# One channel tile of a depthwise convolution: its products on ScalarE instead of GpSimd

## The chip, the cores and the metric

The kernel runs on one core of one Trainium2 chip. The metric is the device time of one execution in microseconds, as the median of several runs. The engines go by the profile's names: PE is TensorE, PEld its weight loads, ACT is ScalarE, DVE is VectorE, POOL (Pool) is GpSimd, SP the engine that issues the transfers.

## What is computed

A two-layer decoder trunk over 1024 tokens of 1024 channels. Layer 0 mixes tokens with a causal convolution module, layer 1 with a gated DeltaNet; behind each mixer stands an MLP with a squared ReLU. The change touches only the convolution of layer 0:

```python
def conformer_conv(h, w_pw1, b_pw1, w_dw, b_dw, ln_g, ln_b, w_pw2, b_pw2):
    u = h @ w_pw1 + b_pw1
    u = jax.nn.glu(u, axis=-1)
    u = causal_depthwise_conv(u, w_dw) + b_dw      # width 31, each channel by itself
    u = jax.nn.silu(layer_norm(u, ln_g, ln_b))
    return u @ w_pw2 + b_pw2

for i in range(DEPTH):
    h = h + mix(rms_norm(h, norm_mix_g[i]))
    h = h + sqrelu_mlp(rms_norm(h, norm_ffn_g[i]), mlp_w1[i], mlp_w2[i])
```

## The kernel before

**Tiles.** Channels stand on the 128 partitions, in 8 channel tiles; the 1024 tokens are done in two halves of 512 (half 0 and half 1). A dense product makes one 128x512 output tile: 8 steps over the input channels, each of three matmuls (L200, L201, L202), because weights and activations are split into a high and a low part (wh, wl; hi, lo) to keep float32's precision. So a product is 24 matmuls. ACT makes the high part of a weight tile (L160), DVE the low part (L161); each of them has two buffers, and the transfers are issued two products ahead, at raised priority (L215).

**The work around the change.** While half 1's convolution runs on DVE, Pool and ACT, PE runs the first MLP of half 0, in four quarters q = 0 to 3 of 8 hidden products (named m1_qo, in full m1_00_qo) and 8 output products (m2_qo). Behind a hidden product, ACT does a ReLU (L573), a square (L574) and the high part of the split (L99), and DVE the low part (L100). Behind an output product, DVE scales (L604, into xo) and adds to h (L357). After the MLP, half 1's second pointwise product (pw2, ps_p) needs the convolution's layer norm.

**The convolution of half 1.** A table, CONV (L30), names for each half and channel tile who does it. A tile of kind "v" is done on DVE alone: 31 multiply-adds (L498), accumulated in PSUM. Kinds "p" and "a" are done by conv_pool (L418): ACT writes the first tap into the sum (L427, cp); then come 30 products of a tap with the shifted input, and 30 adds into the sum on Pool (L437). For "p" the products (cv) are made by Pool (L432), for "a" by ACT (L435). The second number of an entry is the pace: after how many taps the generator yields. In half 1, tiles 0, 1 and 7 go by conv_pool, one after the other; tiles 2 to 6 go by conv_vec on DVE. The products' tiles come from one pool of 27 buffers (GB, L42), which they share with other temporaries.

**What follows a tile.** When a tile is done, conv_done (L405) adds it into a running sum on DVE (L415, ln). When all are, the layer norm (L510) takes the mean over channels with a matmul (L240, mean_lnm), subtracts it on DVE (L519), squares on ACT (L271) and adds up on Pool (L523), takes another matmul (L530, lnv) for the variance, and then 1/sqrt (L246 on ACT, L247 on DVE), a scaling (L542 on DVE, L540 on Pool), Silu twice a tile on ACT (L550, L551) and a split on DVE (L552). Its output tiles (la) share 17 buffers (AB, L41) with the 8 tiles of the MLP's input and 8 hidden tiles, so that all of them are to be had only when the last hidden product of q = 3 has been made.

**What sets the order.** The generators of convolution and layer norm are advanced twice for each dense product (tick, L168). But the order in which each engine gets its instructions is set by the framework's scheduler (the option at L46): it plays the whole program through on a cost model of its own and writes each engine's instructions down in the order in which they would run in it. On the chip each engine keeps to that order, whatever the durations are there. So an edit to one table entry can move instructions on all engines.

Of the kernel before, what the change touches and what calls it, by code (L numbers as in the profile page):

```python
# [27 lines left out]


CONV = ((("a", 2), ("a", 2), ("v", 1), ("v", 2), ("a", 2), ("v", 1), ("s", 1), ("t", 1)),  # L30
        (("p", 1), ("p", 1), ("v", 3), ("v", 1), ("v", 1), ("v", 3), ("v", 1), ("p", 3)))
SHARED = 8
DIAG = 16
WB = 2
# [1184 lines left out]
```

## Time and profile before

| | us |
|---|---|
| median of 3 runs | 2414.03 (2412.52 to 2415.59) |
| the profiled execution | 2410.71 |
| its span in the trace | 2409.0 |
| mean granted clock of PE | 0.986 |
| Pool's work on half 1's convolution ends | 609.45 |
| first matmul of m2_30 (the last hidden product of half 0's first MLP is done) | 607.33 |
| first matmul of half 1's pw2 | 661.63 |

All times in the trace count from the start of the span. A row of the timeline has the start, the duration, engine, line, operation, the tile written and the tiles read, the count if several equal ones follow each other, and in brackets how long the engine had been idle before and what released it. Matmuls overlap their ends, so that the distance of two starts, and not the duration, is the price of one. "Granted clock" is the share of full speed that the clock gate gave PE.

### The profile page before, as it was taken

To read this page: it belongs to the slowest core of one execution; us is meant where nothing else is said; L and a number is where in the kernel's file an instruction comes from. 1 tells how busy PE (TensorE), PEld (TensorE's weight loads), DVE (VectorE), ACT (ScalarE), POOL (GpSimd) and SP (SyncE) were. 2 spreads that over 40 slices of the span, in tenths; PEclk is the share of its full clock that TensorE was granted. 3 is DMA by queue.
4 is the path that set the end of the run, shared out by engine and by line. 5 is a ranking of instruction groups with operands and counts; after the bars stand their busy time and mean duration, and the time that the engine had idled before them with its cause. 6 is when DMAs were issued, how large, how long until landed. Compare 5 with 4: busy or idle time off the path is not lost. (4 is left out here: it accounts for less than half of the span.)

```text
span 2409.0 us, 30448 instructions
## 1 busy us (share of the span) xinstructions
PE 2335.2 (97%) x11484; PEld 1930.9 (80%) x11484; DVE 1594.6 (66%) x2637; ACT 1069.9 (44%) x1566; POOL 574.3 (24%) x414
## 2 busy tenths in 40 slices
PE   8899999999999989999999999899999999999998
PEld 6687778888778878888888888788888887888888
DVE  5797999545868978667444689786775446533334
ACT  6862443243546554352424365544524244432342
POOL 5981399999400110110000000101000000000000
PEclk9898999999999999999999999999999999999999
DMA  8744222333334534333344345343333343433332
GB/s 295 242 166 152 93 88 89 103 96 97 127 114 145 175 112 135 113 120 96 100 140 138 124 138 181 116 128 119 120 97 101 126 132 101 131 96 97 97 104 79
DMA packets 121028, 302.67 MB, mean 126 GB/s; under 512 B 29552, under 2 KB 31792, under 8 KB 120880
## 3 DMA queue, kind: packets, MB, share of 16 engines
q1 hardware_dynamic: 120880, 300.73, 39.0%
q8 instruction: 90, 1.47, 0.3%
q14 instruction: 58, 0.48, 0.1%
HBM read 252.41 MB, written 48.27 MB: 125 GB/s over the span
## 5 line engine op out<-in xcount | busy, mean ns | idle before, releaser
L160 ACT ACTIVATE wh_m<-raw_m 128x1024 fp32r<-128x1024 f32 x256 | 271.4, 1061 | 761.0 <-PE ps_m L201 680.3
L161 DVE TENSOR_TENSOR wl_m<-raw_m,wh_m 128x1024 fp32r<-128x1024 f32 x256 | 327.4, 1279 | 221.2 <-ACT wh_m L160 213.2
L202 PE MATMUL ps_m<-hid,wl_m 128*128 128x512 f32 (+1 forms) x1088 | 414.1, 382 | 10.0 <-DVE wl_m L161 10.0
L200 PE MATMUL ps_m<-hid,wh_m 128*128 128x512 f32 (+1 forms) x1088 | 413.8, 381 | 1.3 <-ACT wh_m L160 0.5
L201 PE MATMUL ps_m<-hid,wh_m 128*128 128x512 f32 (+1 forms) x1088 | 412.1, 380 | 0.0
L437 POOL TENSOR_TENSOR cp<-cp,cv 128x512 f32<-128x512 f32 x187 | 275.4, 1480 | 10.9 <-ACT cv L435 3.7
L202 PEld LDWEIGHTS ps_m<-hid,wl_m 128*128 128x128 f32 x1088 | 205.7, 189 | 49.8 <-DVE wl_m L161 13.4
L200 PEld LDWEIGHTS ps_m<-hid,wh_m 128*128 128x128 f32 x1088 | 205.7, 189 | 39.1 <-ACT wh_m L160 1.8
L201 PEld LDWEIGHTS ps_m<-hid,wh_m 128*128 128x128 f32 x1088 | 205.6, 189 | 36.7 <-issue 0.2
L200 PE MATMUL ps_m<-xn_b,wh_m 128*128 128x512 f32 x512 | 201.4, 393 | 1.0 <-ACT wh_m L160 1.0
L200 PE MATMUL ps_m<-xn_a,wh_m 128*128 128x512 f32 x512 | 200.9, 392 | 1.2 <-ACT wh_m L160 1.2
L201 PE MATMUL ps_m<-xn_a,wh_m 128*128 128x512 f32 x512 | 200.8, 392 | 0.0
L202 PE MATMUL ps_m<-xn_a,wl_m 128*128 128x512 f32 x512 | 200.7, 392 | 0.0
L201 PE MATMUL ps_m<-xn_b,wh_m 128*128 128x512 f32 x512 | 200.6, 392 | 0.0
L202 PE MATMUL ps_m<-xn_b,wl_m 128*128 128x512 f32 x512 | 200.4, 392 | 0.0
L498 DVE SCALAR_TENSOR_TENSOR ca<-u,vec,ca 128x512 f32<-128x512 f32 x268 | 186.1, 743 | 0.4
L432 POOL TENSOR_SCALAR cv<-u,vec 128x512 f32<-128x512 f32 x90 | 174.5, 1946 | 0.0
L1006 POOL TENSOR_TENSOR fof<-fof,rstd_f 128x256 f32<-128x256 f32 x3 | 2.6, 889 | 580.7 <-DVE rstd_f L999 580.7
L800 POOL TENSOR_TENSOR ld<-qe,ld 128x512 f32<-128x512 f32 x16 | 21.6, 1348 | 449.6 <-DVE e L775 274.6
L100 DVE TENSOR_TENSOR hid<-mt,hid 128x512 fp32r<-128x512 f32 x128 | 94.2, 736 | 43.4 <-ACT hid L99 43.2
L200 PEld LDWEIGHTS ps_m<-xn_b,wh_m 128*128 128x128 f32 x512 | 96.2, 188 | 21.7 <-ACT wh_m L160 1.8
L200 PEld LDWEIGHTS ps_m<-xn_a,wh_m 128*128 128x128 f32 x512 | 96.2, 188 | 21.6 <-ACT wh_m L160 2.1
(373 smaller groups left out, 4723.2 us busy)
## 6 DMA issues: line engine op xcount, KB each, us to landing
raw_m<-w SPq DMA_DIRECT2D x256, 512.0 KB, 3.5
raw_in<-w_in SPq DMA_DIRECT2D x64, 512.0 KB, 3.6
sc<-iy SPq DMA_DIRECT2D x64, 256.0 KB, 2.2
ld<-sc SPq DMA_DIRECT2D x64, 256.0 KB, 3.9
raw_p<-w_pw SPq DMA_DIRECT2D x16, 512.0 KB, 3.6
raw_go<-w_out SPq DMA_DIRECT2D x16, 512.0 KB, 3.6
x<-x SPq DMA_DIRECT2D x24, 256.0 KB, 5.4
dh_pa<-wh_pa SPq DMA_DIRECT2D x8, 512.0 KB, 4.0
```

Source lines behind the costliest of these rows:

```text
L100: nc.vector.tensor_tensor(out=dst[:, 1, :], in0=src, in1=dst[:, 0, :].bitcast(F32), op=ALU.subtract)
L160: nc.scalar.activation(out=wh[:, s], in_=raw[:, s], func=AF.Copy)
L161: nc.vector.tensor_tensor(out=wl[:, s], in0=raw[:, s], in1=wh[:, s].bitcast(F32), op=ALU.subtract)
L200: nc.tensor.matmul(o, wh[:, s], hi, start=(k == 0), stop=False)
L201: nc.tensor.matmul(o, wh[:, s], lo, start=False, stop=False)
L202: nc.tensor.matmul(o, wl[:, s], hi, start=False, stop=last)
L432: nc.gpsimd.tensor_scalar(out=t, in0=u[:, j:j + HT], scalar1=tap(ct, j), scalar2=None, op0=ALU.mult)
L437: nc.gpsimd.tensor_tensor(out=c, in0=c, in1=t, op=ALU.add)
L498: nc.vector.scalar_tensor_tensor(out=c if j == CW - 1 else acc, in0=u[:, j:j + HT], scalar=tap(ct, j), in1=acc, op0=ALU.mult, op1=ALU.add)
L800: nc.gpsimd.tensor_tensor(out=qT[h], in0=qe, in1=qT[h], op=ALU.mult)
L1006: nc.gpsimd.tensor_tensor(out=y, in0=y, in1=r, op=ALU.mult)
```

## The change

One entry of CONV: half 1's tile 1 goes from ("p", 1) to ("a", 2). Its 30 products are made by ACT with L435 instead of Pool with L432; its 30 adds stay on Pool; conv_pool yields 15 times for the tile instead of 30. Tiles 0 and 7 stay as they are.

```diff
 CONV = ((("a", 2), ("a", 2), ("v", 1), ("v", 2), ("a", 2), ("v", 1), ("s", 1), ("t", 1)),
-        (("p", 1), ("p", 1), ("v", 3), ("v", 1), ("v", 1), ("v", 3), ("v", 1), ("p", 3)))
+        (("p", 1), ("a", 2), ("v", 3), ("v", 1), ("v", 1), ("v", 3), ("v", 1), ("p", 3)))
```

PE and DVE keep their numbers of instructions, ACT has 30 more and Pool 30 fewer. The order changes on all of them between the first MLP's second quarter and half 1's pw2, from where on it is that of before. Three places, the names read as above (cp1_7 is the convolution's sum of half 1, tile 7; the last number of a name counts instructions):

DVE of the kernel before, where it takes tile 7's sum over, late in q = 3:

```order
L161 TENSOR_TENSOR wl_m1_00_37_4787<-raw_m1_00_37_4784,wh_m1_00_37_4786 128x1024
L100 TENSOR_TENSOR hid_00_35_4780<-mt_00_35_4777,hid_00_35_4780 128x512
L161 TENSOR_TENSOR wl_m2_00_30_4826<-raw_m2_00_30_4823,wh_m2_00_30_4825 128x1024
L415 TENSOR_TENSOR ln1_3117<-ln1_3117,cp1_7_3780 128x512
L100 TENSOR_TENSOR hid_00_36_4819<-mt_00_36_4816,hid_00_36_4819 128x512
L415 TENSOR_TENSOR ln1_3117<-ln1_3117,c1_5_4062 128x512
L161 TENSOR_TENSOR wl_m2_00_31_4870<-raw_m2_00_31_4867,wh_m2_00_31_4869 128x1024
```

DVE of the changed kernel, where it takes the same sum over, in q = 2:

```order
L161 TENSOR_TENSOR wl_m2_00_22_4301<-raw_m2_00_22_4298,wh_m2_00_22_4300 128x1024
L604 TENSOR_TENSOR xo_00_21_4330<-ps_m2_00_21_4304,rstd_r2_2796 128x512
L161 TENSOR_TENSOR wl_m2_00_23_4337<-raw_m2_00_23_4334,wh_m2_00_23_4336 128x1024
L357 TENSOR_TENSOR h01_2147<-h01_2147,xo_00_21_4330 128x512
L415 TENSOR_TENSOR ln1_3117<-ln1_3117,cp1_7_3502 128x512
L604 TENSOR_TENSOR xo_00_22_4366<-ps_m2_00_22_4340,rstd_r2_2796 128x512
L415 TENSOR_TENSOR ln1_3117<-ln1_3117,c1_4_3374 128x512
L357 TENSOR_TENSOR h02_2182<-h02_2182,xo_00_22_4366 128x512
L161 TENSOR_TENSOR wl_m2_00_24_4373<-raw_m2_00_24_4370,wh_m2_00_24_4372 128x1024
```

The sum L415 of cp1_7 stood behind the weight split of m2_30 and ahead of that of m2_31; it now stands ahead of that of m2_24. PE's first matmul with that split is its row 2392 in the one case and 2081 in the other, of a numbering that counts alike in both.

ACT of the kernel before, in q = 1, from the weight split of m1_15 on:

```order
L160 ACTIVATE wh_m1_00_15_3322<-raw_m1_00_15_3320 128x1024
L573 ACTIVATE mt_00_13_3310<-ps_m1_00_13_3281 128x512
L574 ACTIVATE mt_00_13_3310<-mt_00_13_3310 128x512
L99 ACTIVATE hid_00_13_3313<-mt_00_13_3310 128x512
L160 ACTIVATE wh_m1_00_16_3371<-raw_m1_00_16_3369 128x1024
L573 ACTIVATE mt_00_14_3359<-ps_m1_00_14_3326 128x512
L574 ACTIVATE mt_00_14_3359<-mt_00_14_3359 128x512
L99 ACTIVATE hid_00_14_3362<-mt_00_14_3359 128x512
```

ACT of the changed kernel, ahead of and behind the weight split of m1_16:

```order
L574 ACTIVATE mt_00_13_3337<-mt_00_13_3337 128x512
L435 ACTIVATE cv1_1_29_3479<-u1_1_1374,vec_96 128x512
L99 ACTIVATE hid_00_12_3289<-mt_00_12_3286 128x512
L435 ACTIVATE cv1_1_30_3482<-u1_1_1374,vec_96 128x512
L427 ACTIVATE cp1_7_3502<-u1_7_2012,vec_96 128x512
L160 ACTIVATE wh_m1_00_16_3407<-raw_m1_00_16_3405 128x1024
L573 ACTIVATE mt_00_14_3392<-ps_m1_00_14_3356 128x512
L99 ACTIVATE hid_00_13_3340<-mt_00_13_3337 128x512
```

Between a square and a split of the MLP now stand products of tile 1, the last two of which are seen here, and the first tap of tile 7 (L427), directly ahead of the weight split of m1_16. The block of products begins behind the first tap of tile 1, where L574 of m1_11 stood: twelve products, that L574, four products, the weight split of m1_14, and so on. By the semaphores of the built program products 17 and 18 wait for the buffers that Pool's adds 1 and 3 of the tile free, and so on to product 30 (add 14) and the first tap of tile 7 (add 15).

ACT of the changed kernel, at the beginning of q = 3's output products:

```order
L551 ACTIVATE cp1_0_2434<-cp1_0_2434,vec_96 128x512
L551 ACTIVATE cp1_1_3119<-cp1_1_3119,vec_96 128x512
L551 ACTIVATE c1_2_2429<-c1_2_2429,vec_96 128x512
L551 ACTIVATE c1_3_2679<-c1_3_2679,vec_96 128x512
L551 ACTIVATE c1_4_3374<-c1_4_3374,vec_96 128x512
L551 ACTIVATE c1_5_4063<-c1_5_4063,vec_96 128x512
L551 ACTIVATE c1_6_4282<-c1_6_4282,vec_96 128x512
L160 ACTIVATE wh_m2_00_32_4911<-raw_m2_00_32_4909 128x1024
L551 ACTIVATE cp1_7_3502<-cp1_7_3502,vec_96 128x512
L160 ACTIVATE wh_m2_00_33_4953<-raw_m2_00_33_4951 128x1024
```

These are the second Silus of the layer norm (L551), behind the table load and the eight first Silus (L550), which follow L99 of the last hidden product; the weight split of m2_32 stands behind seven of them. In the kernel before the Silus stood behind the weight split of m2_36.

On Pool, the adds of tile 1 stood between its own products; now 17 of them stand one behind the other, and the later ones stand between products of tile 7.

## The prediction, made before the changed kernel was run

> **What bounds the kernel now.** I read the page's table of engines first, then the busy time by stretch over the part of the kernel that the change can reach.
>
> ```profile
> PE 2335.2 (97%) x11484; PEld 1930.9 (80%) x11484; DVE 1594.6 (66%) x2637; ACT 1069.9 (44%) x1566; POOL 574.3 (24%) x414
> 360.00:420.00 60.00, 60.00 (x266) 49.71 (x265) 60.00 (x82) 21.02 (x27) 58.82 (x35) 1.00 0.30 92
> 540.00:600.00 60.00, 60.00 (x266) 49.69 (x265) 33.52 (x32) 22.19 (x29) 59.30 (x35) 1.00 0.31 98
> 640.00:660.00 20.00, 15.11 (x58) 11.68 (x58) 19.00 (x26) 15.20 (x23) 2.31 (x2) 0.91 0.46 146
> ```
>
> In a row by stretch stand the stretch, its length, then busy time and count of PE, PEld, DVE, ACT and Pool, and the granted clock. TensorE is the bound: 97% of the span. Within the first MLP it is gapless (266 matmuls in 60 us, 0.226 us each, so one product of 24 takes 5.44 us). Pool is nearly full there too, while its work is no part of PE's bound; it matters only through who waits for it. PE loses time at 640 to 660. The timeline of PE shows where, and which of its waits DVE's wait for Pool causes:
>
> ```profile
> 542.50 0.39 PE L202 MATMUL ps_m<-hid,wl_m 128*128 128x512 f32 x1
> 607.33 0.39 PE L200 MATMUL ps_m<-hid,wh_m 128*128 128x512 f32 x1
> 611.44 1.12 PE L240 MATMUL mean_lnm<-ln,mean_w 128*128 128x512 f32 x2 [0.77 <-DVE ln L415]
> 643.89 0.39 PE L201 MATMUL ps_m<-hid,wh_m 128*128 128x512 f32 x1
> 646.51 0.50 PE L202 MATMUL ps_m<-hid,wl_m 128*128 128x512 f32 x1 [2.23 <-DVE wl_m L161]
> 651.86 0.40 PE L201 MATMUL ps_m<-hid,wh_m 128*128 128x512 f32 x1
> 654.91 0.69 PE L202 MATMUL ps_m<-hid,wl_m 128*128 128x512 f32 x1 [2.66 <-DVE wl_m L161]
> 655.41 0.63 PE L200 MATMUL ps_m<-hid,wh_m 128*128 128x512 f32 x1
> 655.83 0.63 PE L201 MATMUL ps_m<-hid,wh_m 128*128 128x512 f32 x1
> 658.39 0.43 PE L201 MATMUL ps_m<-hid,wh_m 128*128 128x512 f32 x1
> ```
>
> From 643.89 to 646.51 is 2.62 us where 0.23 was due, from 651.86 to 654.91 it is 3.05: 5.2 us lost. Then from 655.41 to 658.39 seven matmuls start 0.426 us apart, about 1.6 us more for the eight slow ones: 6.8 us in all at 640 to 660, while ScalarE and DVE finish the convolution's layer norm. The wait for the convolution itself (at 611.44) costs 0.8 us. So in the kernel before, Pool's half of the convolution is almost completely hidden. Pool's own rows, and DVE's where it takes Pool's last sum over:
>
> ```profile
> 350.43 1.57 POOL L432 TENSOR_SCALAR cv<-u,vec 128x512 f32<-128x512 f32 x1
> 351.96 1.29 POOL L437 TENSOR_TENSOR cp<-cp,cv 128x512 f32<-128x512 f32 x1
> 367.56 29.20 POOL L437 TENSOR_TENSOR cp<-cp,cv 128x512 f32<-128x512 f32 x16
> 396.75 24.54 POOL L432 TENSOR_SCALAR cv<-u,vec 128x512 f32<-128x512 f32 x14
> 477.33 3.05 POOL L432 TENSOR_SCALAR cv<-u,vec 128x512 f32<-128x512 f32 x1
> 583.03 26.42 POOL L437 TENSOR_TENSOR cp<-cp,cv 128x512 f32<-128x512 f32 x15
> L432 POOL TENSOR_SCALAR cv<-u,vec 128x512 f32<-128x512 f32 x90 | 174.5, 1946 | 0.0
> 609.49 0.69 DVE L415 TENSOR_TENSOR ln<-ln,cp 128x512 f32<-128x512 f32 x1 [5.30 <-POOL cp L437]
> 610.10 0.68 DVE L100 TENSOR_TENSOR hid<-mt,hid 128x512 fp32r<-128x512 f32 x1
> 610.70 0.68 DVE L415 TENSOR_TENSOR ln<-ln,c 128x512 f32<-128x512 f32 x1
> 611.30 1.22 DVE L161 TENSOR_TENSOR wl_m<-raw_m,wh_m 128x1024 fp32r<-128x1024 f32 x1
> ```
>
> Tile 1's work on Pool begins at 396.75 and tile 7's first product at 477.33. Pool ends at 583.03 + 26.42 = 609.45, and 0.04 us later DVE takes the sum, having waited 5.30 us for it, with a weight split (L161) three places behind.
>
> **What the change takes from Pool.** Thirty products L432 leave Pool, at a mean of 1.946 us: 58.4 us. In exchange the adds of tile 1 now wait for ScalarE. That engine's rows at the place:
>
> ```profile
> 401.31 0.62 ACT L574 ACTIVATE mt<-mt 128x512 f32<-128x512 f32 x1
> 410.04 1.06 ACT L160 ACTIVATE wh_m<-raw_m 128x1024 fp32r<-128x1024 f32 x1 [2.56 <-PE ps_m L201]
> 420.92 1.07 ACT L160 ACTIVATE wh_m<-raw_m 128x1024 fp32r<-128x1024 f32 x1 [2.57 <-PE ps_m L201]
> L435 ACT ACTIVATE cv<-u,vec x97: 707/711/725, 39.6 to 177.7; 128x512 f32<-128x512 f32 x97
> ```
>
> In the new order the first of these products stands right behind the start of tile 1's sum (L427), where L574 stood at 401.31. It takes 0.71 us (L435 of half 0), so Pool, free at 396.75, starts at 402.0: 5.3 us idle. Net 53.1 us, and Pool would end at 609.45 - 53.1 = 556.4. That is the value I take. The bounds: the stretch from 477.33 to 609.45 (30 products and 44 adds, 132.1 us) stays; ahead of it stand 16 adds, the number that shared the old stretch with tile 1's products. At 29.20/16 = 1.82 us each, as the row beside a busy DVE has them, they take 29.1 us and Pool ends at 402.0 + 29.1 + 132.1 = 563.2. At 1.29 us (the row at 351.96) they take 20.6 us, and if DVE, standing still in a wait, leaves the last fifteen adds at 1.29 instead of 26.42/15 = 1.76, 7 us more go: 547.7. The difference between the 1.29 and the 1.82 us is a busy DVE. The Trainium skill (GPSIMD Engine Reference, section 8, Key points) says that Pool shares its SBUF interfaces with VectorE and contends with DVE instructions that have two SBUF inputs; these rows agree, and by that rule alone the low end, 547.7, would be the likely one.
>
> **What it moves.** This is where the price lies. The new order brings DVE's sum of tile 7 (L415) forward, from behind the split for product m2_30 to a place ahead of the split for product m2_24; both stand as excerpts with the change. The matmul that needs this split is PE's row 2081, that of m2_31 is row 2392. At 0.2267 us (5.44/24) a row, the 311 rows are 70.5 us, so the demand on Pool comes 70.5 us earlier while Pool is done only 53.1 us earlier. In absolute times: the matmul ran at 542.50 (its row above: 607.33 is row 2367, less 286 rows). DVE needs, after Pool's end, the sum, an L604, another sum, an L357 and the split. By the rows at 609.49 to 611.30 each short one costs 0.60 us and the split 1.22: 0.04 + 4 x 0.60 + 1.22 = 3.7 us. With Pool's end at 556.4 the split is there at 560.1, and PE is 560.1 - 542.5 = **17.6 us** late. DVE processes in order, so the split has no way past the sum; PE, in order too, has no other product to go to. By the bounds: 547.7 gives 8.9 us, 563.2 gives 24.4.
>
> This lateness does not come in one piece. Earlier steps take parts of it, and what they take is then no longer waited for, since Pool's end does not hang on PE. (1) ScalarE: the order puts 16 products and an L574 ahead of the weight split wh of m1_14. From 401.3, 16 x 0.71 + 0.62 = 12.0 us on: it starts at 413.3 instead of 410.04, 3.3 us late. (2) The later products must wait for buffers that Pool's adds free, and the start of tile 7's sum (L427), which needs the buffer of add 15, stands directly ahead of wh of m1_16. Add 15 ends at 402.0 + 15 x 1.82 = 429.3 (421.4 at 1.29), and with 0.8 us for L427 and 1.07 for the split it is there at 431.2 where it was at 422.0: 9.2 us late, or 1.3 by the low price. DVE's split follows it. So PE is about 9 us late from product m1_16 on. (3) DVE's sums of tile 1 and its last steps for tile 4 to 6 are brought forward in the same way, ahead of the splits of m1_26 and m2_20, and wait for Pool's adds too. What remains is taken at m2_24. The sum of all is the 17.6 us, as long as Pool is the latest; if Pool were done by 548, the 9.2 us of ScalarE would be all.
>
> A wait of such length has a follow-up price. Behind the 2.66 us wait at 654.91 the matmuls ran at 0.426 us for eight pieces: 1.6 us, which I add once, behind the last of the waits (the earlier ones are absorbed). The Trainium skill (TensorE: Matmul & The Clock Gate, What's actually happening) has the half clock after an idle window of about 3.4 us; here 2.66 us was enough, so the row decides, and for the longer waits expected here both give the same.
>
> Removed: the 0.8 us wait at 611.44, since the layer norm is now past it by then.
>
> **The layer norm's end.** Its Silu batch can't move up: its tiles come free only with the last hidden product, which ends at PE's 607.33 (T0). In the kernel before the batch comes later and costs the 6.8 us at 640 to 660. ScalarE's rows of it:
>
> ```profile
> 608.27 0.58 ACT L573 ACTIVATE mt<-ps_m 128x512 f32<-128x512 f32 x1
> 609.55 0.63 ACT L99 ACTIVATE hid<-mt 128x512 fp32r<-128x512 f32 x1
> 639.28 1.28 ACT L550 ACT_TABLE_LOAD   x1
> 641.91 2.73 ACT L550 ACTIVATE la<-c,vec 128x512 fp32r<-128x512 f32 x4
> 648.32 2.12 ACT L551 ACTIVATE c<-c,vec 128x512 f32<-128x512 f32 x3
> ```
>
> The new order puts the table load and the first 15 Silus between L99 of m1_37 and wh of m2_32. The batch starts at T0 + 2.9 (609.55 + 0.63), takes 1.28 + 15 x 0.69 (2.73/4 and 2.12/3 lie around it) = 11.6, then the split 1.06: wh is there at T0 + 15.6. PE wants it two products after T0, at T0 + 10.9: about 4.7 us late, 0.5 us more for DVE's part (its split takes 1.22, of which two matmuls run beside it), and 1.6 at the half clock: 6.8 us. So this term is +6.8 - 6.8 = 0. One stall takes the place of the other.
>
> Sum: 17.6 + 1.6 - 0.8 + 0 = **+18.4 us**. The profiled execution is 2410.71 us (span 2409.0 and 1.7 around it), 3.3 us under the median of 2414.03; it would become 2429.1. On the median it is 2432.4. The bounds: 8.9 and 24.4 in place of 17.6 give +9.7 and +25.2, that is 2423.7 and 2439.2; 2 us on each side for the Silu term, which only my reading of the order gives, make 2421.7 to 2441.2.
>
> **Rivals.**
> - *Faster.* Pool runs at its undisturbed prices through the whole stretch: 30 x 1.57 + 44 x 1.29 = 103.9 instead of 132.1 us. Then it ends at 402.0 + 20.6 + 103.9 = 526.5, DVE never waits, and if the Silu batch is hidden as well, the 6.8 and the 0.8 us go: 2414.0 - 7.6 = 2406.4. It decides at a Pool end of 542.5 - 3.7 = 538.8. Against it: products of 3.05 us such as that at 477.33 and the mean of 1.946 stand in the very stretch, and ScalarE's block at m1_16 would also have to vanish. Chance 0.05.
> - *No change.* Pool ends before 538.8 and ScalarE's products fit in, but the Silu batch costs what it cost before: 2414.0 - 0.8 = 2413.2. For it: PE's waits for the convolution total 0.8 us, so there is little that could be won. Chance 0.06.
> - *Slower by ScalarE only.* Pool is done by 548, and the 9.2 us at m1_16 with 1.6 behind it are what counts: 9.2 + 1.6 - 0.8 = +10.0, 2424.0. For it: DVE standing still makes Pool quicker. The Trainium skill's rule on the shared interfaces (GPSIMD Engine Reference, section 8, Key points) speaks for this case. Chance 0.14.
>
> **How the numbers follow.** The forecast (DVE waits for Pool, 2432.4) has 0.75. The range 2422 to 2441 holds it and the third rival; what is left out is the two others, 0.11, and tails of the forecast. A measurement of this kernel can tell about 0.2%, 4.8 us, from no change: below 2409.2 is faster (0.05), up to 2418.9 the same (0.06), above it slower (0.89).
>
> **What would show it.** Right: Pool's last add at about 556 (548 to 563); ScalarE's L435 rows with waits for Pool, and its L160 at 410 and 421 late by 3 and 9 us; DVE's L415 and L498 waiting for Pool in several pieces at 500 to 560, and behind each PE's L202 waiting for DVE's L161 with 0.43 us matmuls after it; 17 to 18 us lost by the end of m2_24, and another 7 us some 11 us after the last hidden product, while the waits at 644 to 655 are gone. Wrong: Pool done before 539; or L415 waiting with PE undisturbed, which would mean that the splits are not behind it; or a loss after pw2 has begun, where the order of all engines is that of before.

## The result and the profile after

The changed kernel took 2435.32 us (median of 4 runs, 2434.89 to 2436.45) against 2413.28 us (4 runs) of the kernel before: a ratio of 1.0083 (95% interval 1.0071 to 1.0095), slower by 22.0 us. Forecast were 18.4 more, 2432.4 us. The profiled execution has a span of 2433.8 us. Each ratio below is against executions of the kernel before that were taken together with it (medians 2413.28 to 2413.97). The medians leave out two executions that ran slowly at a lower granted clock, one of pool_relief (0.912) and the profiled one of tile7_on_act (0.856), so that nothing is read from the latter's trace.

The page's engine row of the changed kernel:

```profile
PE 2344.6 (96%) x11484; PEld 1935.3 (80%) x11484; DVE 1598.0 (66%) x2637; ACT 1088.0 (45%) x1596; POOL 512.9 (21%) x384
```

Pool lost 574.3 - 512.9 = 61.4 us of work and ScalarE took up 18.1; PE, which does the same matmuls, ran slower. Where, the timelines of the changed kernel say. First ScalarE and Pool in q = 1, then Pool's end:

```profile
403.31 7.46 ACT L435 ACTIVATE cv<-u,vec 128x512 f32<-128x512 f32 x12
410.67 0.62 ACT L574 ACTIVATE mt<-mt 128x512 f32<-128x512 f32 x1
411.19 2.54 ACT L435 ACTIVATE cv<-u,vec 128x512 f32<-128x512 f32 x4
413.64 1.04 ACT L160 ACTIVATE wh_m<-raw_m 128x1024 fp32r<-128x1024 f32 x1
...
427.67 0.82 ACT L427 ACTIVATE cp<-u,vec 128x512 f32<-128x512 f32 x1 [0.41 <-POOL cp L437]
428.39 1.04 ACT L160 ACTIVATE wh_m<-raw_m 128x1024 fp32r<-128x1024 f32 x1
```

```profile
404.10 26.62 POOL L437 TENSOR_TENSOR cp<-cp,cv 128x512 f32<-128x512 f32 x17 [6.78 <-ACT cv L435]
...
532.72 25.41 POOL L437 TENSOR_TENSOR cp<-cp,cv 128x512 f32<-128x512 f32 x15
```

The split of m1_14 begins at 413.64 and that of m1_16 at 428.39, both without a wait. In the kernel before these two were ScalarE's rows:

```profile
404.60 1.06 ACT L160 ACTIVATE wh_m<-raw_m 128x1024 fp32r<-128x1024 f32 x1 [2.01 <-PE ps_m L201]
...
415.48 1.06 ACT L160 ACTIVATE wh_m<-raw_m 128x1024 fp32r<-128x1024 f32 x1 [2.56 <-PE ps_m L201]
```

So they come 9.0 and 12.9 us later. (The rows at 410.04 and 420.92, which the prediction shows, are the splits of m1_15 and m1_17.) Pool ends at 532.72 + 25.41 = 558.13 instead of 609.45. Then DVE, in the three places of the order where it waits for Pool and, further on, where the layer norm's scaling stands ahead of a split:

```profile
519.10 1.18 DVE L415 TENSOR_TENSOR ln<-ln,cp 128x512 f32<-128x512 f32 x1 [7.10 <-POOL cp L437]
520.20 1.21 DVE L161 TENSOR_TENSOR wl_m<-raw_m,wh_m 128x1024 fp32r<-128x1024 f32 x1
...
531.25 2.31 DVE L498 SCALAR_TENSOR_TENSOR c<-u,vec,ca 128x512 f32<-128x512 f32 x3 [5.99 <-POOL cp L437]
...
558.16 0.69 DVE L415 TENSOR_TENSOR ln<-ln,cp 128x512 f32<-128x512 f32 x1 [5.31 <-POOL cp L437]
558.77 0.68 DVE L604 TENSOR_TENSOR xo<-ps_m,rstd_r 128x512 f32<-128x512 f32 x1
...
560.57 1.22 DVE L161 TENSOR_TENSOR wl_m<-raw_m,wh_m 128x1024 fp32r<-128x1024 f32 x1
...
587.72 3.35 DVE L247 RECIPROCAL rstd_ln<-rstd_ln 128x512 f32<-128x512 f32 x1
591.10 1.89 DVE L542 SCALAR_TENSOR_TENSOR cp<-cp,vec,rstd_ln 128x512 f32<-128x512 f32 x1
592.91 5.19 DVE L542 SCALAR_TENSOR_TENSOR c<-c,vec,rstd_ln 128x512 f32<-128x512 f32 x3
598.03 1.21 DVE L161 TENSOR_TENSOR wl_m<-raw_m,wh_m 128x1024 fp32r<-128x1024 f32 x1
```

Each of these waits or blocks ends in a weight split, and PE's timeline of the changed kernel has the answer to each:

```profile
414.74 0.50 PE L200 MATMUL ps_m<-xn_a,wh_m 128*128 128x512 f32 x1 [2.51 <-ACT wh_m L160]
417.12 0.79 PE L202 MATMUL ps_m<-xn_a,wl_m 128*128 128x512 f32 x1 [1.65 <-DVE wl_m L161]
...
431.86 0.50 PE L202 MATMUL ps_m<-xn_a,wl_m 128*128 128x512 f32 x1 [0.76 <-DVE wl_m L161]
...
521.47 0.50 PE L202 MATMUL ps_m<-xn_a,wl_m 128*128 128x512 f32 x1 [1.54 <-DVE wl_m L161]
...
535.13 0.50 PE L202 MATMUL ps_m<-hid,wl_m 128*128 128x512 f32 x1 [2.45 <-DVE wl_m L161]
...
561.84 0.50 PE L202 MATMUL ps_m<-hid,wl_m 128*128 128x512 f32 x1 [1.70 <-DVE wl_m L161]
...
599.29 0.50 PE L202 MATMUL ps_m<-xn_a,wl_m 128*128 128x512 f32 x1 [1.84 <-DVE wl_m L161]
...
648.34 0.79 PE L200 MATMUL ps_m<-hid,wh_m 128*128 128x512 f32 x1 [4.07 <-DVE h L357]
```

The waits are short, since an earlier one always takes a part of the next. What counts is PE's lateness against the kernel before. The table gives it for this kernel and for the experiments below: the start of an instruction (ReLU L573 of a hidden product, DVE's L604 of an output product, first matmul of pw2) in that trace less its start in the trace of before, less the same difference at the last hidden product of q = 0, in us (one execution each; outside this stage two executions differ by 1 to 2 us).

| kernel | end of q = 1 | end of q = 2 | last hidden product of q = 3 | pw2 |
|---|---|---|---|---|
| changed | 10.0 | 20.6 | 25.3 | 22.5 |
| sums_held | 10.3 | 13.6 | 13.6 | 11.9 |
| pool_relief | 1.8 | 6.6 | 9.8 | 6.3 |
| held_no_block | 9.4 | 11.1 | 11.1 | 9.4 |
| one_input_spread | 1.0 | 0.7 | 0.7 | -2.5 |
| one_input_block | 7.2 | 7.9 | 7.9 | 6.1 |
| tile7_held | 1.9 | 11.0 | 11.0 | 9.4 |
| tile7_held_early | 1.9 | 11.0 | 12.7 | 12.2 |
| only_adds | 7.6 | 7.1 | 7.1 | 5.6 |
| only_one_input | 0.9 | 0.4 | 0.4 | -1.1 |

The changed kernel loses 10 us in q = 1, 10.6 in q = 2 (some 2 of which are the layer norm's mean matmuls, which stand there now and not behind q = 3) and 4.7 in q = 3 (0.9 of them the variance's matmuls, L530, moved in the same way); it gets 2.8 back behind it, as these matmuls and their wait are gone there.

Of q = 1's 10 us, 1.4 are not the change's: behind a wait of 2.06 us, which both traces have at 355 us, PE is at half the clock (granted 0.50) up to 358 us in the trace of before and up to 361 us in this one. The runs pool_relief, one_input_block, tile7_held and only_one_input have the same 1.4 us in the table; sums_held and only_adds don't. Another 2.7 us are a half clock behind the wait at 417.12: the 14 matmuls from there to 422.83 start 0.44 us apart.

One stall has replaced the other at the end: the two waits for the splits of m2_36 and m2_37 are gone, and 4.46 us lie between 643.88 and 648.34, ahead of m2_32. (The brackets name what came last by semaphore, L357; the split wh of m2_32 ended at 648.29.)

### The profile page after: what moved, and what is told of

Same layout as the page of the kernel before. It is cut to its first block, busy times and chain, and to the rows that moved or that the text cites. A ratio compares the mean times of both kernels' runs of the same rounds, so it can differ in the third digit from the quotient of the medians.

```text
span 2433.8 us, 30398 instructions
## 1 busy us (share of the span) xinstructions
PE 2344.6 (96%) x11484; PEld 1935.3 (80%) x11484; DVE 1598.0 (66%) x2637; ACT 1088.0 (45%) x1596; POOL 512.9 (21%) x384
## 5 line engine op out<-in xcount | busy, mean ns | idle before, releaser
L437 POOL TENSOR_TENSOR cp<-cp,cv 128x512 f32<-128x512 f32 x187 | 274.6, 1475 | 21.0 <-ACT cv L435 12.7
L202 PEld LDWEIGHTS ps_m<-hid,wl_m 128*128 128x128 f32 x1088 | 206.5, 190 | 49.6 <-DVE wl_m L161 12.9
L100 DVE TENSOR_TENSOR hid<-mt,hid 128x512 fp32r<-128x512 f32 x128 | 97.3, 760 | 47.5 <-ACT hid L99 47.2
L202 PEld LDWEIGHTS ps_m<-xn_a,wl_m 128*128 128x128 f32 x512 | 97.2, 190 | 27.6 <-DVE wl_m L161 7.5
L432 POOL TENSOR_SCALAR cv<-u,vec 128x512 f32<-128x512 f32 x60 | 114.7, 1918 | 0.0
```

Of the source, the lines that this page charges most:

```text
L100: nc.vector.tensor_tensor(out=dst[:, 1, :], in0=src, in1=dst[:, 0, :].bitcast(F32), op=ALU.subtract)
L202: nc.tensor.matmul(o, wl[:, s], hi, start=False, stop=last)
L432: nc.gpsimd.tensor_scalar(out=t, in0=u[:, j:j + HT], scalar1=tap(ct, j), scalar2=None, op0=ALU.mult)
L437: nc.gpsimd.tensor_tensor(out=c, in0=c, in1=t, op=ALU.add)
```

## The experiments

Theory A was the prediction's: DVE's in-order waits for Pool set PE's lateness, and ScalarE's block only takes a part of it in advance. Its rivals: the block is all (B), or the earlier layer norm is (C).

**Holding DVE's steps back.** The scheduler can be made to place an instruction later only by a true dependency. So a tiny operation is added ahead of the sums of tiles 1 and 7 and of the last taps of tiles 4 to 6: it adds zero times a column that exists only once a product of q = 3 is made.

```diff
+    def hold(c, n):
+        while len(go) < n:
+            yield
+        nc.vector.scalar_tensor_tensor(out=c[:, 0:1], in0=go[n - 1], scalar=0.0, in1=c[:, 0:1],
+                                       op0=ALU.mult, op1=ALU.add)
...
+            elif hf and ct:
+                ends.append((ct, c))
             else:
                 conv_done(hf, ct, c)
+        for ct, c in ends:
+            if ct:
+                yield from hold(c, 1 + ct // 7)
+            conv_done(hf, ct, c)
...
+                if hf and j == CW - 1 and ct > 3:
+                    yield from hold(acc, 1)
...
+            if (l, hf) == (0, 0) and (q, o) in ((3, 1), (3, 5)):
+                go.append(sp.tile([P, 1], F32, tag=f"go{o}", name=f"go{o}"))
+                nc.vector.tensor_copy(go[-1], t[:, 0:1])
```

> The changed kernel, with DVE's steps that need Pool held back: seven tiny DVE operations (one column, times zero, added to the sum; or the copy of a column that the others read) make the sums of tiles 1 and 7 and the last taps of tiles 4 to 6 wait for a product of q = 3, so that they stand in DVE's order where they stood before the change (ahead of the splits of m1_34 and m2_30). ScalarE's block in q = 1 stays as in the changed kernel. Theory A (DVE's in-order waits for Pool set PE's lateness, and ScalarE's block only takes a part of it in advance): the steps at m1_26, m2_20 to m2_24 and m1_32 go, ScalarE's 10 us in q = 1 stay: about 2423 us. Rival B (ScalarE's block is the whole price): no change from the changed kernel, about 2435. Rival C (the price is the layer norm that runs earlier, at m1_32 and in front of m2_32): all gone but nothing of q = 1 mattering, about 2413.

Measured: 2421.12 us, ratio 1.0034 (1.0022 to 1.0046); forecast by A was 2423. The waits of DVE in this kernel, from 490 to 610 us, with what they waited for:

```profile
DVE wl_m L161 <- ACT wh_m L160: 38.3, 13, 3.8
DVE xo L623 <- PE ps_m L209: 20.1, 7, 4.8
DVE hid L100 <- ACT hid L99: 6.4, 11, 0.6
```

None for Pool is left, and 14.2 of the 22.0 us are gone: of the table's lateness at pw2 10.6, the rest of the medians' difference lying outside this stage, where single executions differ by 1 to 2 us ahead of it and as much behind. The 10 us of q = 1 stay. In q = 2 3.3 us are left, behind a wait of 2.08 us at 542.07 for a split that took DVE 2.29 us. That B and C are each not all of it is shown by this one run. It can't tell A from C in what is gone, as holding the sums back also puts the layer norm back to its old place; that is read from the rows above, where DVE waits for Pool, and from the next run.

**Pool's relief alone.** Pool's products of tile 1 fall away, and nobody makes them.

```diff
-                t = g_tile(f"cv{hf}_{ct}_{j}")[:, :HT]
+                t = g_tile(f"cv{hf}_{ct}_{j}")[:, :HT] if how == "p" or not hf else u[:, j:j + HT]
...
-                else:
+                elif not hf:
```

> Pool's relief alone: tile 1's 30 products of half 1 are made by nobody (its adds take the shifted input itself), so Pool has the 30 fewer instructions of the changed kernel and ScalarE has no block. DVE's sum of tile 7 stands ahead of the split of m2_25. Theory A: Pool has no idle time for ScalarE and ends at about 551, the split of m2_25 comes at about 555 where 548 was due, so 7 us, with the 3.5 us that the changed kernel loses at m1_32: about 2423. Rival B: 2413 or less. Rival C: only the 3.5 us, about 2417.

Measured: 2418.38 us, 1.0027 (1.0017 to 1.0036). DVE waits for Pool and PE for DVE, with no product on ScalarE at all:

```profile
549.75 2.56 DVE L415 TENSOR_TENSOR ln<-ln,cp 128x512 f32<-128x512 f32 x2 [4.54 <-POOL cp L437]
```

```profile
553.81 1.12 PE L240 MATMUL mean_lnm<-ln,mean_w 128*128 128x512 f32 x2 [2.10 <-DVE ln L415]
```

Pool's end is at 551, as forecast, and the lateness of 6.6 us at the end of q = 2 is A's first term (7 us). Of the 3.2 more in q = 3 (3.5 forecast) 1.4 are the wait at m1_32, the rest is for the most part the variance's matmuls and their wait. But 3.5 us come back behind q = 3, which the forecast of 2423 left out, so that the time lies nearer to C's 2417. C has no wait for Pool, though, and the rows show one. So to take 58 us of work from Pool and give it to nobody makes this kernel slower, by 5.0 us in the median and 6.5 by the ratio: the scheduler moves the demand further forward than Pool gets faster.

**Another tile, and no block.** Tile 7 in place of tile 1 (`("p", 1)` for tile 1 and `("a", 3)` for tile 7), and the held version of the changed kernel with tile 0's sum deferred too (`elif hf:` in place of `elif hf and ct:`).

> Tile 7 instead of tile 1 gets its products from ScalarE (tile 1 stays with Pool, pace 3 as it was). ScalarE's products then stand four or five to a weight split, from m1_23 to m2_21, with no block; DVE's sum of tile 7 stands ahead of the split of m2_25. Theory A: Pool ends at about 551, 5 to 7 us late at m2_25, and 3.5 us at m1_32: about 2422. Rival B: no block, so 2413. Rival C: 2417.

> The held-back sums as in the run with the block, and tile 0's sum deferred with them, which in the built order lets tile 1's work begin in the quarter before and spreads ScalarE's products to three to five a weight split. Theory A: nothing waits for Pool and nothing blocks ScalarE, Pool ends some 50 us ahead of its use: 2413, within 3 us, of which the loss at the end of the layer norm is the same as before. Rivals B and C: 2413 too; over 2420 would speak against all three.

Measured: tile7_on_act 2433.27 us (three executions), 1.0082 (1.0065 to 1.0099), about as slow as the changed kernel; held_no_block 2421.88, 1.0031 (1.0019 to 1.0042). Both miss every theory. In held_no_block 9 us are lost by the end of q = 1, 2.2 of them already in q = 0's output products, where its adds begin. Pool's adds, DVE's weight splits from 396 to 432 us, and the busy time of q = 1 (PE, PEld, DVE, ACT, Pool) in it:

```profile
381.84 48.60 POOL L445 TENSOR_TENSOR cp<-cp,cv 128x512 f32<-128x512 f32 x30 [9.96 <-ACT cv L443]
```

```profile
L161 DVE TENSOR_TENSOR wl_m<-raw_m,wh_m 128x1024 fp32r<-128x1024 f32 x6 | 12.3, 2054 | 0.0
```

```profile
360.00:420.00 60.00, 55.77 (x239) 45.05 (x238) 60.00 (x71) 31.52 (x45) 49.96 (x32) 0.98 0.27 82
```

The same group in the kernel before:

```profile
L161 DVE TENSOR_TENSOR wl_m<-raw_m,wh_m 128x1024 fp32r<-128x1024 f32 x7 | 9.0, 1283 | 0.7 <-ACT wh_m L160 0.7
```

DVE is full (60.00 of 60 us, as before the change), and its splits take 2.05 us instead of 1.28 beside thirty adds in a row: it gets 71 instructions done instead of 82. PE's waits from 375 to 436 us are all for it, while ScalarE waits for Pool:

```profile
PE ps_m L209 <- DVE wl_m L161: 6.1, 5, 2.4
ACT cv L443 <- POOL cp L445: 12.0, 15, 1.5
```

That made theory D: two-input adds on Pool slow DVE's two-input steps, and a full DVE hands that on to PE.

**Testing D.** First on the two held versions with ScalarE's products, where tile 1's adds become one-input operations, and on tile 7's version with the sums held back, whose adds stand beside a DVE that is half idle:

```diff
-                nc.gpsimd.tensor_tensor(out=c, in0=c, in1=t, op=ALU.add)
+                if (hf, ct) == (1, 1):
+                    nc.gpsimd.tensor_scalar(out=c, in0=t, scalar1=tap(ct, j), scalar2=None,
+                                            op0=ALU.mult)
+                else:
+                    nc.gpsimd.tensor_tensor(out=c, in0=c, in1=t, op=ALU.add)
```

> The run without block and with held sums, but tile 1's 30 adds on Pool are replaced by 30 one-input multiplications of the product's tile (the sum of tile 1 is left out). That run lost 9 us in q = 1 with ScalarE's products spread evenly; its weight splits on DVE took 2.05 us each beside Pool's back-to-back adds, where they take 1.28 beside Pool's products in the kernel before, on a DVE that was busy 60.00 of 60 us already. Theory D (two-input adds on Pool, one behind the other, slow DVE's two-input steps, and a full DVE passes that on to PE): the splits return to about 1.3 us, q = 1 loses 1 to 2 us, about 2414. Rival E (ScalarE's extra products as such delay the MLP's own steps): the 9 us stay, about 2421.

> The same replacement (tile 1's sum left out) in the run with held sums and ScalarE's block of 16 products ahead of the weight split of m1_14. Theory D alone: 2414 here too. Rival F (the block, with the fourteen convolution taps that stand ahead of DVE's split of m1_14 in the new order, and the wait of tile 7's first tap for Pool ahead of m1_16): the 8 us stay, about 2421. Between them, the difference to 2421 is the part of the slowed DVE.

> Tile 7 instead of tile 1 gets its products from ScalarE, with the sums and last taps held back as in the other runs. Its adds stand beside m1_23 to m2_21, where DVE was busy 28 to 34 of 60 us in the kernel before, and ScalarE's products four or five to a split. Theories A and D: neither a wait for Pool nor a full DVE: 2413, within 3 us. Rival E: 2421, with the loss in q = 2.

Measured: tile7_held 2421.13 us, 1.0035 (1.0024 to 1.0047): a miss in size. Against tile7_on_act, holding the sums back is worth 12 us (14 in the changed kernel), as theory A has it, of the 20 us which that run lost; but 9 us are lost in q = 2, and ScalarE's timeline of tile7_held shows how:

```profile
501.05 0.72 ACT L443 ACTIVATE cv<-u,vec 128x512 f32<-128x512 f32 x1 [0.32 <-POOL cp L445]
502.75 0.72 ACT L443 ACTIVATE cv<-u,vec 128x512 f32<-128x512 f32 x1 [0.97 <-POOL cp L445]
503.38 1.04 ACT L160 ACTIVATE wh_m<-raw_m 128x1024 fp32r<-128x1024 f32 x1
...
509.83 1.04 ACT L160 ACTIVATE wh_m<-raw_m 128x1024 fp32r<-128x1024 f32 x1
```

Pool's row there:

```profile
486.37 70.61 POOL L445 TENSOR_TENSOR cp<-cp,cv 128x512 f32<-128x512 f32 x43 [7.33 <-ACT cv L443]
```

Each weight split stands behind four products (the last two of the first four are shown) whose buffers Pool's adds must free, at 70.61/43 = 1.64 us an add: 4 x 1.64 = 6.6 us, and the two splits are 6.45 us apart where PE asks for one each 5.44. In order, ScalarE hands Pool's pace on to PE. This is rival E in a sharper form (the products delay the MLP's steps, but by what they wait for); it is read from the trace and was not tested by itself.

Of the other two, one_input_spread took 2411.61 us, 0.9988 (0.9979 to 0.9998), 10 us less than its twin with adds, and one_input_block 2419.36, 1.0028 (1.0017 to 1.0040), 1.8 us less than sums_held. So ScalarE's block, with the convolution taps that stand ahead of DVE's split of m1_14 in that order, is most of q = 1's loss in the changed kernel (7.2 of 10 us by the table, both with the 1.4 us that are not the change's). That the slowed DVE is the rest is only likely: the 1.8 us lie within the two intervals, and the two orders differ on ScalarE and DVE. Without the block the slowed DVE seemed to be all. That last reading has a flaw: the order of one_input_spread puts two to four products ahead of a split and not three to five, so it also relaxes ScalarE's coupling to Pool. A pair without ScalarE settles it: no products for tiles 1 and 7 (`("a", 3)` for tile 7 and the edit of pool_relief, sums held), once with 60 adds and once with 60 one-input operations (the test above with `hf and ct`), and the same order of PE, DVE and ScalarE in both.

> No products at all for tiles 1 and 7 of half 1 (nobody makes them; the adds take the shifted input itself, so both tiles' sums are wrong), with the sums held back. Pool then has 60 two-input adds one behind the other from about 397 on, beside a DVE that is full until about 430, and ScalarE has no product and waits for nothing of Pool's. Theory D (the adds slow DVE's two-input steps): DVE's splits in q = 1 take 1.7 to 2.1 us and PE loses 5 to 9 us there: 2419 to 2423. Rival G (in the runs before it was ScalarE, standing in its order behind products that wait for Pool's buffers, that paced PE): nothing is lost in q = 1: 2413.

> The twin: the same 60 places on Pool hold one-input multiplications instead of adds (tile 1's and tile 7's sums are left out); the orders of PE, DVE and ScalarE are the same row for row. Theory D: splits at 1.2 to 1.3 us and nothing lost, 2413, so that the pair differs by 5 to 9 us. Rival G: both alike.

Measured: 2414.03 us, 1.0006 (0.9996 to 1.0015), and 2410.21, 0.9983 (0.9974 to 0.9992): 3.8 us apart in the medians and 5.5 by the ratios, where 5 to 9 were forecast and the table has 7.6 against 0.9 us in q = 1. Neither level is the one forecast, as only_adds can't be told from the kernel before; why is open. Pool's row, DVE's splits from 396 to 480 us, and the busy time of the second half of it, of only_adds:

```profile
401.55 92.72 POOL L445 TENSOR_TENSOR cp<-cp,u 128x512 f32<-128x512 f32 x60 [4.79 <-ACT cp L435]
```

```profile
L161 DVE TENSOR_TENSOR wl_m<-raw_m,wh_m 128x1024 fp32r<-128x1024 f32 x14 | 26.4, 1886 | 0.0
```

```profile
420.00:480.00 60.00, 57.25 (x243) 46.27 (x242) 46.05 (x40) 16.84 (x21) 60.00 (x40) 0.97 0.29 96
```

and of only_one_input:

```profile
402.88 108.07 POOL L446 TENSOR_SCALAR cp<-u,vec 128x512 f32<-128x512 f32 x60 [6.18 <-ACT cp L435]
```

```profile
L161 DVE TENSOR_TENSOR wl_m<-raw_m,wh_m 128x1024 fp32r<-128x1024 f32 x16 | 19.6, 1226 | 5.3 <-ACT wh_m L160 5.2
```

```profile
420.00:480.00 60.00, 60.00 (x265) 49.42 (x265) 30.38 (x38) 16.94 (x20) 60.00 (x34) 1.00 0.29 97
```

Pool is busy all the time in both, and it is DVE that pays: 1.89 us for a split beside adds and 1.23 beside one-input operations, 46 us of work in 60 instead of 30. So D is shown, and G alone is not what happened. In held_no_block, too, DVE is without a gap from 375 to 436 us and never waits for ScalarE, so that ScalarE's 12.0 us of waiting for Pool don't reach PE there; in tile7_held, where DVE does wait for ScalarE, they do, by the rows above. The slowing is not of all of DVE's work: three multiply-adds into PSUM take 2.06 us in both kernels of the pair (beginning at 415.65 in only_adds, at 411.10 in only_one_input), while L100, which like the split reads two tiles, takes 1.48 us instead of 0.68.

**Towards a faster kernel.** The first try holds tile 7's version one and three products less, with (3, 0) and (3, 2) in place of (3, 1) and (3, 5); the others leave CONV as before and let the idle Pool copy the high part of a Silu instead of computing it a second time, for all tiles (first diff) or the odd ones (second):

```diff
-            if k % 2 and small:
+            if k % 2 or not small:
```

```diff
-            if k % 2 and small:
+            if k % 2:
```

> The same, held two or three products less (until the first and the third hidden product of q = 3), so that the layer norm's statistics fall into q = 3 and the Silus stand between the splits of m2_32 to m2_34 instead of m2_35 to m2_37. If Pool is done in time (551 to 560), the layer norm's loss of 6.8 us at its end shrinks, as the Silus now have the weight splits of m2_32 and m2_33 between them: 2407 to 2412. If seven Silus ahead of the split of m2_32 are still too many: 2413.

> The kernel before, with the second Silu of all eight tiles of half 1's layer norm as the only one (in place, in float32) and its high part copied by Pool, idle there: eight ScalarE operations of about 0.69 us fewer between the splits of m2_36 and m2_37, eight Pool copies more. If ScalarE's Silus are what PE waits for at 644 to 655 (6.8 us): 2407 to 2410. If the copies (each over 1 us on one engine) make DVE's last splits late: 2413 or more.

> The same for the four odd tiles alone, as half 0 does it: four ScalarE operations fewer and four Pool copies. Half of the gain, 2410 to 2412, if ScalarE's work sets the loss.

Measured: tile7_held_early 2422.84 us, 1.0044 (1.0029 to 1.0059). It has tile7_held's loss in q = 2, and the Silus are still too many ahead of the split of m2_32; PE's row there:

```profile
634.74 0.79 PE L207 MATMUL ps_m<-hid,wh_m 128*128 128x512 f32 x1 [4.62 <-DVE h L364]
```

before_pool_copies 2410.82 us, 0.9986 (0.9977 to 0.9995), faster than both kernels by 3.2 us and more, if by less than forecast; before_half_copies 2412.51, 0.9995 (0.9986 to 1.0004), not to be told from before. In the first, PE's two waits of 2.23 and 2.66 us have become one, for a split that DVE reaches at 649.08:

```profile
650.72 0.77 PE L202 MATMUL ps_m<-hid,wl_m 128*128 128x512 f32 x1 [3.79 <-DVE wl_m L161]
```

```profile
642.03 4.50 DVE L542 SCALAR_TENSOR_TENSOR c<-c,vec,rstd_ln 128x512 f32<-128x512 f32 x3
...
649.08 1.58 DVE L161 TENSOR_TENSOR wl_m<-raw_m,wh_m 128x1024 fp32r<-128x1024 f32 x1
```

DVE works there without a gap, with the layer norm's scaling (L542) ahead of the split. ScalarE waits for Pool's scalings (1.31 and 1.42 us for L540), but its half of that weight is done at 643.35, and Pool's copies begin only at 644.91.

In that one trace the stage gains 1.4 us (its lateness falls from 2.6 at the end of q = 3's hidden products to 1.2 at pw2); where the other 1.8 us of the medians come from is open.

## Why the prediction was right, point by point

- **Pool's end: right.** 558.13 us where 556.4 was taken. Pool was idle for 6.78 us, not 5.3 (ScalarE came to the first product later by the 1.4 us above), and the 17 adds behind it took 26.62/17 = 1.57 us each, between the two bounds. The prediction put the difference of the bounds down to a busy DVE, but DVE is without a gap beside the add of 1.29 us at 351.96 too. What it is busy with counts, as the pair of runs shows from DVE's side.
- **The demand 70.5 us earlier, and the lateness at m2_24: right.** The split was there at 561.79, 3.7 us behind Pool's end, and the matmul that ran at 542.50 ran at 561.84. Less the 0.6 us that this execution was late from the start, that is 18.7 us for the 17.6. That this wait is the cause rests on three things: the rows, in which DVE waits for Pool ahead of the split; pool_relief, where the same happens without a product on ScalarE; and sums_held, where the wait is gone and 10.6 us of lateness with it.
- **The parts that earlier steps take: right in size, in part by luck.** PE was 10 us late by the end of q = 1 (9.2 forecast at m1_16), of which the longer half clock at 355 us made 1.4 and the one behind 417.12 some 2.7; neither was in the forecast. Two rows were misread: 410.04 and 420.92 are the splits of m1_15 and m1_17, not of m1_14 and m1_16. The sum bears it, since there are two buffers and a split begins when PE is done with the product two before it, so that these rows also mark when PE turns to m1_14 (410.07) and m1_16. The forecast had ScalarE's products wait for buffers; in the trace only L427 waits (0.41 us), and the block is work: thirty products of 0.63 us between the MLP's steps. And a part is the slowed DVE (its split of m1_14 took 2.35 us; 1.8 us by the medians of sums_held and one_input_block, which is not clear of their intervals), which the prediction didn't see. It had the contention of Pool and DVE as a price on Pool's adds alone, and cited the Trainium skill (GPSIMD Engine Reference, section 8, Key points) for it. The pair of runs agrees with that rule where Pool adds, with 1.89 us for DVE's split against 1.23 beside one-input operations, and there the price falls on DVE.
- **The half clock behind the last wait, 1.6 us: wrong place.** Behind 561.84 there was none; only 1.70 us of the wait were left there. There was one behind the 2.45 us wait at 535.13, which the next wait for Pool absorbed, and one behind the 1.84 us wait at 599.29.
- **Missing: m1_32.** The reciprocal (3.35 us) and the scaling of four tiles (1.89 and 5.19 us) stand on DVE between the splits of m1_31 and m1_32 in the new order, and cost 1.84 us of waiting and about 1.6 at the half clock. The prediction counted nothing there. pool_relief shows the step without ScalarE's products: 1.43 us of waiting at 585.96, and no half clock behind it.
- **The layer norm's end, 0: nearly right.** The 0.8 us wait at the mean is gone, as forecast. At 643.88 to 654.85 the changed kernel loses 4.2 us of waiting and some 3.3 at the half clock, 7.5 for the 6.8 of before and of the forecast (a second wait of 0.44 us, at 649.99, is in the 3.3).

Sum: 18.7 - 0.8 + 3.4 + 0.7 = 22.0 us, where the table has 22.5 at pw2 and the medians differ by 22.0; single executions differ by more than that, so the agreement to the tenth is luck. It is luck, too, that the 1.6 us which the forecast of 18.4 has in the wrong place stand in for half of what it left out at m1_32. The two rivals on the faster side fell at the point named for them: Pool would have had to end by 538.8. The third, slower by ScalarE only, has its mechanism in the changed kernel, but what it costs is covered by the later wait: sums_held, which removes that wait, comes out at +7.8 us.

## What to carry to other kernels

When the order of the engines is written down beforehand from a cost model, an edit's price is where the model and the chip disagree: here the order asked for Pool's result 70 us earlier, and Pool delivered it 51 us earlier. Look up what is queued behind each first use of a slow engine's result, on an engine that works in order, before counting what the slow engine saves. Work taken off an engine that hardly anything waits for has next to nothing to win, and may still cost, when it changes what stands behind what elsewhere.

## What the runs showed of the hardware

- Two-input adds on Pool, one behind the other, make DVE's two-input splits take 1.89 us (only_adds) to 2.05 us (held_no_block), one-input operations leave them at 1.23 us. Which of the two engines pays differs: in the kernel before, sixteen adds took 1.82 us each from 367.56 on with DVE's splits at 1.21 to 1.78, in only_adds 1.55 us each with the splits slowed. The runs don't show why.
- On Pool a one-input multiplication by a column is the longer operation: 108.07/60 = 1.80 us against 92.72/60 = 1.55 for an add of two tiles.
- The half clock followed a wait of only 1.84 us (599.29), beginning 1.3 us behind it, but not a wait of 2.23 us (646.51 of the kernel before). Nor does it always last as long: behind the same wait of 2.06 us at 355 us it ended at 358 us in one trace and at 361 to 362 us in another, which is 1.4 us of time. PE's rows in the changed kernel:

```profile
599.29 0.50 PE L202 MATMUL ps_m<-xn_a,wl_m 128*128 128x512 f32 x1 [1.84 <-DVE wl_m L161]
...
600.55 0.58 PE L201 MATMUL ps_m<-xn_a,wh_m 128*128 128x512 f32 x1
600.93 0.63 PE L202 MATMUL ps_m<-xn_a,wl_m 128*128 128x512 f32 x1
...
603.49 0.63 PE L202 MATMUL ps_m<-xn_a,wl_m 128*128 128x512 f32 x1
```

The eight matmuls from 600.55 to 603.49 start 0.42 us apart, where 0.23 is the rule.
